# Block products of a gated network: sums of the seven products made by two wide additions, and one more pair of tiles in each network

## The chip, the cores and the metric

The kernel runs on one core of a Trainium2 chip. The metric is device time in microseconds (us) of one execution, the median of several runs. One further execution is recorded by the hardware profiler, and its trace is what the profile shows. Engines: PE (TensorE: matmuls; PEld is its weight load), DVE (VectorE), ACT (ScalarE), POOL (GpSimd) and SP (SyncE, which here issues DMAs).

## The reference, cut to what matters

Two residual layers on x of 512 tokens by 1024 channels. Each has a token mixer (first a state-space layer, then forgetting attention) and a gated network. The change lies in the two gated networks:

```python
def conv_ffn(h, w_up, conv_w, conv_b, w_down):
    up = h @ w_up
    a, b = jnp.split(up, 2, axis=-1)
    ...
    a_conv = conv_b
    for i in range(CONV_W):
        a_conv = a_conv + ap[:, i:i + S] * conv_w[i]
    return (jax.nn.silu(a_conv) * b) @ w_down
```

Here h is 512 by 1024 (normalised and modulated), w_up is 1024 by 5632, the convolution is causal with width 3 along the tokens, and w_down is 2816 by 1024.

## The kernel before, in words

Channels lie on the 128 partitions and tokens along the free dimension. All numbers are float32. To keep the precision, both operands of a matmul are split into a high part (rounded to the matmul's input format by a copy on ACT, line 301) and a low part (the difference, by a subtraction on DVE, line 302), and a product is three matmuls: high times high, high times low, low times high (lines 317 and 587).

The 2816 channels are 22 **pairs** of tiles: pair f is tile 2f (the half that is convolved) and tile 2f + 1 (the half that multiplies it). A pair is computed in one of two ways, chosen in `ffn` by the tuple `plain`, which lists the plain pairs.

- **Plain** (`product`, line 318): each tile is 8 blocks of 128 input channels, by three matmuls, of 512 tokens each: 24 matmuls of 512 columns, 48 a pair.
- **By block products** (`quarters`, lines 547 to 618): the pair's weights are seen as a 2 by 2 matrix of blocks, a11, a12 (the two halves of tile 2f's input channels) and a21, a22 (those of tile 2f + 1), and x as blocks b11, b12, b21, b22 (halves of the channels, by halves of the tokens, t1 and t2). Seven products of half the channels and half the tokens do in place of eight, after the method of Strassen and Winograd, with sums of weights s1 = a21 + a22, s2 = s1 - a11, s3 = a11 - a21, s4 = a12 - s2 and sums of x t1 = b12 - b11, t2 = b22 - t1, t3 = b22 - b12, t4 = t2 - b21. Each product is 12 matmuls of 256 columns. The four sums of weights are four DVE operations of 512 columns, and a11 with a12, s1 with s2, s4 with s3, and a22 are split into parts (three splits of 1024 columns and one of 512). The sums of x and their parts are made once in each network by `forms_x`, between the plain pairs at its start, ahead of the first pair by block products.

The results are: tile 2f is a11·b11 + a12·b21 for the first tokens and a11·b11 + s2·t2 + s1·t1 + s4·b22 for the second; tile 2f + 1 is a11·b11 + s2·t2 + s3·t3 - a22·t4 and a11·b11 + s2·t2 + s3·t3 + s1·t1. In PSUM, p1 gathers a11·b11, then s2·t2, then s3·t3, and p5 gathers s1·t1, then s4·b22. Since p1 and p5 go on gathering, what they hold in between is copied out by ACT (`copy`, line 594): after a11·b11, after s1·t1 and after s2·t2; p4 is copied as well. DVE then adds in four operations of 256 columns, each with one operand in PSUM (lines 607, 611, 616, 617, all recorded at line 555). `p1`, `p5`, `p2` and `p4` are in four PSUM tiles, of which the left half is used: two from `mm`, two from `aux` (four banks each). `oa` and `ob`, the sums in SBUF, share two buffers under the name nm_t.

`finish` is `gated`, lines 633 to 656: tile 2f is convolved (ACT at line 637, twice DVE at 639, ACT's Silu at 642), tile 2f + 1 multiplies it (DVE, 649), and the product is split into ghi and glo for w_down.

The pairs are in groups (`QGROUPS`, one tuple for each network). While the pairs of group q are computed, the products with w_down of group q - 1 are put between them (`down`, line 693): eight tiles of output a group, each with 3 matmuls of 512 columns for every pair in the group, spread evenly over the pairs of the next group. The first group has none between its pairs; those of the last group come at the end (line 696). Their results are added to the residual stream h by DVE (line 400).

The order on each engine in this part isn't written out by hand. Instructions carry the order of the program as priority, and a scheduler lays out each engine's queue ahead of time, by its own model of durations, letting a later instruction go ahead of one that isn't ready. On the chip each queue then runs in that order. `behind` (lines 182 to 187) adds waits for the order's sake: the parts of a pair's weights come after the copy of s2·t2 of the pair before (`self.copied`).

In network 1 DVE also makes 24 sums for the modulation of later layers (line 271), some after each product (`tick`). Weights come by DMA from SP's queue into three buffers named raw (in network 1 those of w_down into one named rawd).

Lines that the change and the prediction touch: 43 (`QGROUPS`), 301 and 302 (splits), 318 (plain products and w_down), 513 to 545 (`forms_x`), 547 to 618 (`quarters`), 633 to 656 (`gated`), 676 to 696 (the loop over pairs), 1797 and 1811 (the two networks, with `plain`).

Of the kernel before, what the change touches and what calls it, by code (L numbers as in the profile page):

```python
# [9 lines left out]
F32 = mybir.dt.float32  # L10
F32R = mybir.dt.float32r
I32 = mybir.dt.int32
AF = mybir.ActivationFunctionType
ALU = mybir.AluOpType
# [4 lines left out]
P = 128  # L19
D = 1024  # L20
KT = D // P
S = 512
# [17 lines left out]
WARM = 11  # L40

GROUPS = (11, 11)
QGROUPS = ((4, 4, 5, 4, 5), (6, 5, 6, 5))
TAIL = 6
FIRST = (("c", (KT,)), ("s5_prm", (3, G // 2)), ("s5_eye", (64,)), ("s5_causal", (L,)))
REST = (
# [27 lines left out]
def part_of(pool, shape, name, tag, bufs, aside=0):  # L74

    _, n, w = shape
    t = pool.tile([P, ROOM if bufs == WB else n * w + P], F32R, name=name, tag=tag, bufs=bufs)
    return t[:, aside:aside + n * w].rearrange("p (n w) -> p n w", w=w)


class Trunk:
# [465 lines left out]
    def quarters(self, pool, l, f, x, finish):  # L547

        nc = self.nc
        H, N = KT // 2, S // 2  # L550
        t1, t2 = HALVES
        a, b = (self.raw([P, KT, P], self.io["w_up"][l][2 * f + j]) for j in range(2))
        a11, a12, a21, a22 = a[:, :H], a[:, H:], b[:, :H], b[:, H:]
        c, d = (pool.tile([P, 2, H, P], F32, name="sums", bufs=2) for _ in range(2))
        sub = lambda o, u, v, op=ALU.subtract: nc.vector.tensor_tensor(o, u, v, op)  # L555
        w = {}
        copied = self.copied

        def parts(src, names, *where):
            hi, lo = (  # L560
                pool.tile([P, H * P + P], F32R, name=n, tag="e" + n)[:, ASIDE:ASIDE + H * P].rearrange("p (n w) -> p n w", w=P)
                if where else part_of(self.wpool, [P, len(names) * H, P], n, n, WB, ASIDE)
                for n in ("w_hi", "w_lo")
            )
            with self.behind(*copied):
                self.put_parts(hi, lo, src)
            for j, n in enumerate(names):
                w[n] = hi[:, j * H:(j + 1) * H], lo[:, j * H:(j + 1) * H]

        parts(a, ("a11", "a12"))  # L570
        sub(c[:, 0], a21, a22, ALU.add)
        sub(c[:, 1], c[:, 0], a11)
        parts(c.rearrange("p n k m -> p (n k) m"), ("s1", "s2"))
        sub(d[:, 1], a11, a21)
        sub(d[:, 0], a12, c[:, 1])
        parts(d.rearrange("p n k m -> p (n k) m"), ("s4", "s3"))
        parts(a22, ("a22",), pool)
        quarter = lambda k, t: tuple(v[:, k * H:(k + 1) * H, t] for v in x)
        xs = {"b11": quarter(0, t1), "b21": quarter(1, t1), "b22": quarter(1, t2)}
        for n, v in self.tx.items():  # L580
            xs[f"t{n}"] = v

        def times(o, wn, xn, first=True):
            (whi, wlo), (xhi, xlo) = w[wn], xs[xn]
            for k in range(H):
                for n, (wt, xt) in enumerate(((whi, xhi), (whi, xlo), (wlo, xhi))):
                    self.last_mm = nc.tensor.matmul(  # L587
                        o, wt[:, k], xt[:, k], start=(first and k == 0 and n == 0), stop=(k == H - 1 and n == 2),
                        skip_group_check=True,
                    )  # L590

        def copy(o, last=False):
            t = self.tmp.tile([P, N], F32, name="nm_h", bufs=4)
            a = nc.scalar.activation(t, o, AF.Copy)  # L594
            if last:
                self.copied = [a.ins]
            return t

        p1, p5 = (self.mm.tile([P, S], F32, name="mmp")[:, :N] for _ in range(2))
        p2, p4 = (self.aux.tile([P, S], F32, name="aux")[:, :N] for _ in range(2))  # L600
        oa, ob = (self.tmp.tile([P, S], F32, name="nm_t") for _ in range(2))
        times(p1, "a11", "b11")
        c1 = copy(p1)
        times(p5, "s1", "t1")
        c5 = copy(p5)
        times(p2, "a12", "b21")
        sub(oa[:, t1], p2, c1, ALU.add)
        times(p1, "s2", "t2", False)
        c2 = copy(p1, True)
        times(p5, "s4", "b22", False)  # L610
        sub(oa[:, t2], p5, c2, ALU.add)
        finish(2 * f, oa, slice(0, S))
        times(p4, "a22", "t4")
        c4 = copy(p4)
        times(p1, "s3", "t3", False)
        sub(ob[:, t2], p1, c5, ALU.add)
        sub(ob[:, t1], p1, c4)
        finish(2 * f + 1, ob, slice(0, S))

    def ffn(self, i, l, x, nxt, ticks=0, plain=None):  # L620

        nc, tc = self.nc, self.tc
        with tc.tile_pool(name=f"ffn{l}", bufs=1, reuse_waits="tile") as pool:
# [4 lines left out]
            cw, cb = conv[:, :3], conv[:, 3]  # L628
            groups = QGROUPS[l] if plain else GROUPS
            first = [sum(groups[:q]) for q in range(len(groups) + 1)]  # L630
# [86 lines left out]
class Ew:  # L717
# [29 lines left out]
    def sub(self, a, b, out=None):  # L747
        return self.tt(a, b, ALU.subtract, out)
# [1040 lines left out]
def build(tc, io, out, stop=None):  # L1789
    with ExitStack() as ctx:  # L1790
        k = Kernel(tc, io, ctx)
        x = k.s5(0, k.norm_mod(1))
        if stop == "s5":
            return k.dump(out)
        k.done()
        k.bg = [k.ada_units(units(*((2, t) for t in range(3))))]
        x = k.ffn(1, 0, x, k.norm_mod(2), ticks=1, plain=(0, 1, 2, 3, 6))
        k.done()
        k.bg = [
            k.ada_units(units((3, 1))[:7], rooms=("s3", "phi", "plo"), late=False),  # L1800
            k.ada_units(units((3, 1))[7:] + units((3, 0))[:6], rooms=(1, 2), late=False),
            k.ada_units(units((3, 0))[6:], rooms=("s3", "nf"), late=False),
        ]
        if stop == "ffn0":
            return k.dump(out)
        x = k.fox(2, x, k.norm_mod(3))
        k.done()
        k.mods.close()
        if stop == "fox":
            return k.dump(out)  # L1810
        k.ffn(3, 1, x, k.norm_out(out), plain=(0, 1, 2, 3))
        k.finish_norm()


# [81 lines left out]
```

## Time and profile before

| | |
|---|---|
| median of 3 runs | 1204.44 us (1204.01 to 1206.35) |
| profiled execution | 1204.63 us, of which its span, first to last instruction, 1202.8 us |
| granted PE clock, mean | 0.998 |
| pairs by block products | 17 in network 1 (plain: 0, 1, 2, 3, 6), 18 in network 2 (plain: 0 to 3) |
| network 1, about | 250 to 600 us of the span |
| network 2, about | 850 to 1200 us |

A row of a timeline gives start and duration in us, the engine, the line of the kernel, the operation, the tiles (output<-inputs) with their shapes, and a count; in brackets stands the idle time ahead of it with what ended it. Matmuls are pipelined and their ends are modelled, so PE's pace is read from starts. A row of a group ends with the busy time in us, the mean duration in ns, and the engine's idle time just ahead of these instructions with what ended most of it. A row of waits gives the total in us, the number of times and the longest.

### The profile page before, as it was taken

What the parts mean: (1) busy time and instruction counts of PE and PEld (TensorE: products, weight loads), DVE (VectorE), ACT (ScalarE), POOL (GpSimd) and SP (SyncE); (2) the same over time, 40 slices, a digit from 0 to 9 for tenths busy, and PEclk for the clock granted to TensorE, in tenths of its full rate; (3) what the DMA queues carried; (4) which work ended last, traced back from release to release, by engine and by line L of the source; (5) the groups of instructions that cost most, each with busy time, mean ns of one, the idle gap of its engine ahead of it and who ended that gap; (6) DMA issues with size and microseconds to landing.
All of it is one profiled execution on the core that took longest, in us unless ns stands there. A gap on an engine that the chain in (4) does not pass through costs nothing.

```text
span 1202.8 us, 20697 instructions
## 1 busy us (share of the span) xinstructions
PE 1179.2 (98%) x7947; PEld 1019.3 (85%) x7947; DVE 1010.3 (84%) x1843; ACT 615.7 (51%) x1179; POOL 124.5 (10%) x230
## 2 busy tenths in 40 slices
PE   9999999999999999999999999999999999999997
PEld 4576677898988899999899787878989999999987
DVE  8889887879899999998786678876899888888865
ACT  3565544436545544555452566664456555555543
POOL 3221011100000000000000344430000000000000
PEclk9999999999999999999999999999999999999999
DMA  9598677821465455433444444433123342323331
GB/s 370 190 348 282 197 247 253 280 71 53 142 191 162 143 169 181 142 112 88 140 169 167 150 149 150 142 113 102 59 70 97 123 125 86 110 88 110 112 100 71
DMA packets 71826, 182.00 MB, mean 151 GB/s; under 512 B 23103, under 2 KB 24479, under 8 KB 70703
## 3 DMA queue, kind: packets, MB, share of 16 engines
q1 hardware_dynamic: 58479, 136.63, 35.2%
q0 software_dynamic: 11920, 43.26, 10.6%
q8 instruction: 62, 1.02, 0.3%
q10 hardware_dynamic: 1328, 0.79, 0.2%
q14 instruction: 37, 0.30, 0.1%
HBM read 173.73 MB, written 6.92 MB: 150 GB/s over the span
## 4 chain that ended last, share of the span: by engine, by line
PE 60%; issue 19%; DVE 10%; DMA 7%; ACT 2%; POOL 1%; SPq 0%; DVEq 0%; POOLq 0%; ACTq 0%
PE mmp L318 25%; PE mmp L587 14%; PE aux L587 5%; PE mmp L1276 4%; DVE w_lo L302 3%; PE mmp L1616 2%; DMA raw<-in_ada_w 2%; PE aux L1034 1%; PE aux L1755 1%; DMA raw<-in_w_up 1%; PE mmp L227 1%; PE aux L1146 1%; PE aux L1775 1%; DMA ada_raw<-in_ada_t 1%; DMA rawd<-in_w_down 1%
## 5 line engine op out<-in xcount | busy, mean ns | idle before, releaser
L302 DVE TENSOR_TENSOR w_lo<-raw,w_hi 128x1024 fp32r<-128x1024 f32 (+4 forms) x173 | 186.1, 1080 | 26.5 <-ACT w_hi L301 26.1
L301 ACT ACTIVATE w_hi<-raw 128x1024 fp32r<-128x1024 f32 (+4 forms) x173 | 154.0, 899 | 86.7 <-PE mmp L318 35.4
L318 PE MATMUL mmp<-ghi,w_hi 128*128 128x512 f32 (+1 forms) x412 | 147.7, 359 | 0.7 <-DVE h L400 0.7
L318 PE MATMUL mmp<-ghi,w_lo 128*128 128x512 f32 (+1 forms) x412 | 147.3, 357 | 1.1 <-DVE w_lo L302 1.1
L318 PE MATMUL mmp<-glo,w_hi 128*128 128x512 f32 (+1 forms) x412 | 147.2, 357 | 0.0
L318 PE MATMUL mmp<-a_hi,w_hi 128*128 128x512 f32 (+1 forms) x320 | 116.5, 367 | 1.5 <-ACT a_hi L470 1.5
L587 PE MATMUL mmp<-w_hi 128*128 128x256 f32 x420 | 116.2, 277 | 0.8 <-ACT w_hi L301 0.4
L587 PE MATMUL mmp<-w_hi,w_lo 128*128 128x256 f32 x420 | 116.0, 277 | 0.0
L587 PE MATMUL mmp<-w_lo,w_hi 128*128 128x256 f32 x420 | 116.0, 276 | 0.0
L318 PE MATMUL mmp<-a_hi,w_lo 128*128 128x512 f32 (+1 forms) x320 | 114.3, 358 | 0.0
L318 PE MATMUL mmp<-a_lo,w_hi 128*128 128x512 f32 (+1 forms) x320 | 114.0, 357 | 0.0
L302 DVE TENSOR_TENSOR w_lo<-sums,w_hi 128x1024 fp32r<-128x1024 f32 x78 | 94.8, 1218 | 0.0
L301 ACT ACTIVATE w_hi<-sums 128x1024 fp32r<-128x1024 f32 x78 | 81.0, 1055 | 23.3 <-DVE sums L555 21.8
L594 ACT ACTIVATE nm_h<-mmp 128x256 f32<-128x256 f32 x105 | 39.6, 381 | 103.1 <-PE mmp L587 103.0
L318 PEld LDWEIGHTS mmp<-ghi,w_lo 128*128 128x128 f32 x412 | 77.4, 188 | 13.5 <-DVE w_lo L302 1.9
L318 PEld LDWEIGHTS mmp<-ghi,w_hi 128*128 128x128 f32 x412 | 77.3, 188 | 11.5 <-issue 0.9
L318 PEld LDWEIGHTS mmp<-glo,w_hi 128*128 128x128 f32 x412 | 77.4, 188 | 10.3
L587 PEld LDWEIGHTS mmp<-w_hi 128*128 128x128 f32 x420 | 78.8, 188 | 1.4 <-ACT w_hi L301 0.7
L587 PEld LDWEIGHTS mmp<-w_hi,w_lo 128*128 128x128 f32 x420 | 78.7, 188 | 0.4 <-DVE w_lo L302 0.2
L587 PE MATMUL mmp<-a_hi,w_hi 128*128 128x256 f32 x280 | 77.9, 278 | 1.1 <-ACT nm_h L594 0.9
L587 PEld LDWEIGHTS mmp<-w_lo,w_hi 128*128 128x128 f32 x420 | 78.8, 188 | 0.0
L587 PE MATMUL mmp<-a_hi,w_lo 128*128 128x256 f32 x280 | 77.7, 277 | 1.1 <-DVE w_lo L302 1.0
(339 smaller groups left out, 3128.3 us busy)
## 6 DMA issues: line engine op xcount, KB each, us to landing
raw<-in_w_up SPq DMA_DIRECT2D x88, 512.0 KB, 4.0
ada_raw<-in_ada_t POOLq DMA_DIRECT2D x40, 512.0 KB, 4.1
raw<-in_ada_w POOLq DMA_DIRECT2D x24, 512.0 KB, 6.3
nf<-nfd SPq DMA_DIRECT2D x8, 1152.0 KB, 7.0
raw<-in_ada_w SPq DMA_DIRECT2D x16, 512.0 KB, 9.8
raw<-in_fox_qk SPq DMA_DIRECT2D x16, 512.0 KB, 3.5
raw<-in_w_down SPq DMA_DIRECT2D x24, 320.0 KB, 3.0
rawd<-in_w_down SPq DMA_DIRECT2D x24, 256.0 KB, 3.4
```

The source lines that it names most:

```text
L227: self.last_mm = nc.tensor.matmul(ps[32 * qq:32 * qq + 32, :], self.sc32[:, k, :], w[:, q * S:(q + 1) * S], start=(step is steps[0]), stop ...
L301: self.rounded = nc.scalar.activation(hi, src, AF.Copy).ins
L302: return nc.vector.tensor_tensor(lo, src, hi.bitcast(F32), ALU.subtract)
L318: self.last_mm = self.nc.tensor.matmul(o if len(xt.shape) == 2 else by_place(o), wt, xt, start=(k == 0 and n == 0), stop=(k == nk - 1 and ...
L587: self.last_mm = nc.tensor.matmul(o, wt[:, k], xt[:, k], start=(first and k == 0 and n == 0), stop=(k == H - 1 and n == 2), skip_group_che ...
L594: a = nc.scalar.activation(t, o, AF.Copy)
L1034: nc.tensor.matmul(ps[:, :, cols], x[:, q, r].rearrange("p c j -> p (c j)"), both[:, :, planes, q, :], start=(r == 0), stop=(r == 1), skip ...
L1146: self.nc.tensor.matmul(yp[g2][:, k, 1:], w2[rows, k, r].rearrange("p c i -> p (c i)"), st[rows, r, k, :B - 1], start=False, stop=(r == 1) ...
L1276: one = lambda k: nc.tensor.matmul(ps, w[m][:, k, :], x[:, k], start=(k == 0), stop=(k == KT - 1))
L1616: self.last_mm = nc.tensor.matmul(ps[q, b][:, :n], xt[:, k, tb], wt, start=(k == 0 and i == 0), stop=(k == KT - 1 and i == 2),)
L1755: nc.tensor.transpose(pt[:, r - rs[0], k, :], s[:, r, k * P:(k + 1) * P], self.ident)
L1775: nc.tensor.matmul(pv[:, c * P:], self.v[:, hp, k, r].rearrange("p t d -> p (t d)"), pp[:, r, c + 3 * k:NB + 3 * k, :].rearrange("p b t -> ...
```

## The change

Three edits. In `quarters`, p2 and p5 become the two halves of one PSUM tile u, and p4 and p1 the two halves of one tile v; ACT copies straight into `oa` and `ob` (p4 with its sign turned), and two DVE operations of 512 columns make the sums in place, the second with p1 read twice by a broadcast. The four additions of 256 columns and the four small SBUF tiles of the copies go. In each network one pair more goes by block products: pair 6 in network 1, pair 3 in network 2. The groups of network 2 become 4, 6, 6, 6 pairs.

```diff
-QGROUPS = ((4, 4, 5, 4, 5), (6, 5, 6, 5))
+QGROUPS = ((4, 4, 5, 4, 5), (4, 6, 6, 6))
...
-        def copy(o, last=False):
-            t = self.tmp.tile([P, N], F32, name="nm_h", bufs=4)
-            a = nc.scalar.activation(t, o, AF.Copy)
-            if last:
-                self.copied = [a.ins]
-            return t
-
-        p1, p5 = (self.mm.tile([P, S], F32, name="mmp")[:, :N] for _ in range(2))
-        p2, p4 = (self.aux.tile([P, S], F32, name="aux")[:, :N] for _ in range(2))
+        def copy(t, o, scale=1.0):
+            return nc.scalar.activation(t, o, AF.Copy, scale=scale).ins
+
+        u, v = self.mm.tile([P, S], F32, name="mmp"), self.aux.tile([P, S], F32, name="aux")
+        p2, p5 = u[:, t1], u[:, t2]
+        p4, p1 = v[:, t1], v[:, t2]
         oa, ob = (self.tmp.tile([P, S], F32, name="nm_t") for _ in range(2))
         times(p1, "a11", "b11")
-        c1 = copy(p1)
+        copy(oa[:, t1], p1)
         times(p5, "s1", "t1")
-        c5 = copy(p5)
-        times(p2, "a12", "b21")
-        sub(oa[:, t1], p2, c1, ALU.add)
+        copy(ob[:, t2], p5)
+        times(p2, "a12", "b21", False)
         times(p1, "s2", "t2", False)
-        c2 = copy(p1, True)
+        self.copied = [copy(oa[:, t2], p1)]
         times(p5, "s4", "b22", False)
-        sub(oa[:, t2], p5, c2, ALU.add)
+        sub(oa, u, oa, ALU.add)
         finish(2 * f, oa, slice(0, S))
-        times(p4, "a22", "t4")
-        c4 = copy(p4)
+        times(p4, "a22", "t4", False)
+        copy(ob[:, t1], p4, -1.0)
         times(p1, "s3", "t3", False)
-        sub(ob[:, t2], p1, c5, ALU.add)
-        sub(ob[:, t1], p1, c4)
+        halves = lambda t: t.rearrange("p (n w) -> p n w", w=N)
+        sub(halves(ob), p1[:, None, :].to_broadcast([P, 2, N]), halves(ob), ALU.add)
         finish(2 * f + 1, ob, slice(0, S))
...
-        x = k.ffn(1, 0, x, k.norm_mod(2), ticks=1, plain=(0, 1, 2, 3, 6))
+        x = k.ffn(1, 0, x, k.norm_mod(2), ticks=1, plain=(0, 1, 2, 3))
...
-        k.ffn(3, 1, x, k.norm_out(out), plain=(0, 1, 2, 3))
+        k.ffn(3, 1, x, k.norm_out(out), plain=(0, 1, 2))
```

## The prediction

> **What bounds the kernel now.** The page comes first: its span, and the busy share of each engine.
>
> ```profile
> span 1202.8 us, 20697 instructions
> ...
> PE 1179.2 (98%) x7947; PEld 1019.3 (85%) x7947; DVE 1010.3 (84%) x1843; ACT 615.7 (51%) x1179; POOL 124.5 (10%) x230
> ```
>
> PE carries the span, with DVE close behind. The profiled execution took 1204.63 us, 1.8 us more than its span; the median of the runs shown is 1204.44 us, so a sum made against the one holds for the other. Next, PE's order of time where a plain tile ends and a block product begins (start, duration, engine, line, tiles, shapes).
>
> ```profile
> 297.16 0.39 PE L318 MATMUL mmp<-a_hi,w_lo 128*128 128x512 f32 x1
> ...
> 299.88 0.39 PE L318 MATMUL mmp<-a_hi,w_lo 128*128 128x512 f32 x1
> ...
> 301.37 0.28 PE L587 MATMUL mmp<-w_hi 128*128 128x256 f32 x1
> ...
> 302.73 0.28 PE L587 MATMUL aux<-a_hi,w_hi 128*128 128x256 f32 x1
> ```
>
> Durations overlap, so starts count. Twelve matmuls of 512 columns take 2.72 us, 0.2267 each; twelve of 256 columns 1.36 us, 0.1133 each. A plain pair has 48 of the first, 10.88 us; a pair by block products has 7 x 12 of the second, 9.52 us. **Each pair that changes over is worth 1.36 us of PE**, if PE has no wait. The windows by stage (length, busy time of PE, PEld, DVE, ACT, POOL with instructions, granted clock, DMA) tell where it hasn't.
>
> ```profile
> 320.00:340.00 20.00, 20.00 (x111) 17.32 (x110) 14.55 (x23) 7.20 (x11) 1.06 (x2) 1.00 0.66 217
> ...
> 400.00:420.00 20.00, 18.29 (x131) 16.69 (x129) 19.19 (x33) 11.64 (x20) 1.58 (x3) 1.00 0.38 123
> ...
> 880.00:900.00 20.00, 20.00 (x98) 16.69 (x97) 19.45 (x23) 9.95 (x14) 0.00 (x0) 1.00 0.25 71
> ```
>
> The first row is where network 1 now has its plain pair 6: DVE has 5.4 us to spare. In the second, DVE is 96% busy and PE loses 1.7 us. The last is the start of network 2: DVE is 97% busy, while plain pairs still keep PE full. PE is the bound, and DVE is as good as a second one in these places.
>
> **The change, part by part.** DVE's prices are read from starts in its order of time.
>
> ```profile
> 327.07 0.75 DVE L555 TENSOR_TENSOR nm_t<-mmp,nm_h 128x256 f32<-128x256 f32 x2
> 327.74 1.22 DVE L302 TENSOR_TENSOR w_lo<-raw,w_hi 128x1024 fp32r<-128x1024 f32 x1
> ...
> 334.28 1.29 DVE L555 TENSOR_TENSOR sums<-raw 128x512 f32<-128x512 f32 x2
> 335.48 0.69 DVE L555 TENSOR_TENSOR sums<-sums,raw 128x512 f32<-128x512 f32 x1
> ...
> 340.78 0.69 DVE L302 TENSOR_TENSOR w_lo<-rawd,w_hi 128x512 fp32r<-128x512 f32 x1 [2.74 <-ACT w_hi L301]
> ...
> 344.32 1.22 DVE L302 TENSOR_TENSOR w_lo<-sums,w_hi 128x1024 fp32r<-128x1024 f32 x1
> 345.46 0.68 DVE L649 TENSOR_TENSOR conv<-conv,mmp 128x512 f32<-128x512 f32 x1
> 346.06 1.22 DVE L302 TENSOR_TENSOR w_lo<-sums,w_hi 128x1024 fp32r<-128x1024 f32 x1
> ```
>
> *Two additions for four.* Now a pair has four additions of 256 columns, 0.34 us each from start to start (0.67 for the two); a 512-column operation with an operand in PSUM takes 0.60 (345.46 to 346.06). Two of those are 1.20 against 1.34: 0.14 us less DVE work in a pair, 5 us over the 35 pairs there are. PE waits for none of it directly, so I count it at nothing by itself. The broadcast operand of the second addition is in no row; between 0.60 and the 0.67 of two halves it doesn't matter. The copies on ACT stay four, of the same size.
>
> [...]
>
> *One more pair by block products in each network.* It takes two weight splits of 1024 away (2 x 1.14 us; 1.14 from 344.32 to 345.46) and brings three of 1024, one of 512 (0.60), four sums of 512 (0.60 each) and the two additions: 7.6 for 2.3, **5.3 us more DVE work** for 1.36 us less PE work.
>
> In network 1 it falls on pair 6. The 5.4 us of idle DVE take the work up, 2.74 us of it in the row at 340.78. But the stretch of the second window row comes right behind, where DVE is the bound, and DVE ends no earlier because PE arrives 1.36 us earlier. I count the gain there as given back, -1.36 + 1.36 = 0; bounds -1.4 (all taken up) and +2.6 (half of the 5.3 late).
>
> In network 2 the pair moved is number 3, the last plain one before block products begin.
>
> ```profile
> 890.33 1.22 DVE L302 TENSOR_TENSOR w_lo<-sums,w_hi 128x1024 fp32r<-128x1024 f32 x1
> 891.46 2.35 DVE L302 TENSOR_TENSOR w_lo<-raw,w_hi 128x1024 fp32r<-128x1024 f32 x2
> 893.73 0.74 DVE L639 SCALAR_TENSOR_TENSOR conv<-mmp,conv_wb,conv 128x511 f32<-128x511 f32 x1
> ...
> 897.46 1.23 DVE L302 TENSOR_TENSOR w_lo<-sums,w_hi 128x1024 fp32r<-128x1024 f32 x1
> ```
> ```profile
> 897.64 0.39 PE L318 MATMUL mmp<-a_hi,w_lo 128*128 128x512 f32 x1
> 897.87 0.28 PE L587 MATMUL mmp<-a_lo,w_hi 128*128 128x256 f32 x1
> ```
>
> The row at 890.33 splits the last of the four sums of x (forms_x); until then DVE is full. Plain pair 3 ends on PE at 897.87, so pair 2 ends 10.88 us before, at 887.0. There PE would now need pair 3's block weights, and nothing else is at hand: the first group has no products of w_down behind it. Without the two plain splits of 1.14 the forms are done near 890.3. From the end of the last plain split (891.46 + 2 x 1.14, less the block pair's first split: 892.6) to s1's low part at 898.7 lie 6.1 us, of which 1.3 are the two steps of another pair's convolution (the first is the row at 893.73): 4.8. So s1 is ready near 895.1, and from there six products (8.16 us) run to 903.2, where the plain pair ended at 897.87: **+5.3 us**. If DVE makes pair 3's weights ahead of the last two forms (4 x 1.14 us earlier) it is +0.8. The trace's order follows the program's, forms first; I take +4.
>
> *One bank for two products.* p2 and p5 now lie in one tile, p4 and p1 in another. Twice in a pair PE writes into a tile from which ACT is still copying the other half: p2 behind the copy of p5, s3·t3 behind the copy of p4. No row has this case. If order goes by columns it costs nothing. If it goes by tile, PE waits for the copy. One row of PE's waits has it held for a copy out of the tile that it writes, so I take the latter.
>
> ```profile
> PE mmp L587 <- ACT nm_h L594: 1.2, 2, 0.9
> ```
> ```profile
> 302.93 0.39 ACT L594 ACTIVATE nm_h<-mmp 128x256 f32<-128x256 f32 x1 [0.45 <-PE mmp L587]
> ```
>
> [...]
>
> This is the copy behind s1·t1, whose last matmul started at 302.62 (one before 302.73): it ends at 303.32, and the next product starts at 302.73 today. So p2 would start 0.6 us late, 37 x 0.6 = 22 us, unless PE has other work. It has: s2·t2 goes to the other tile, and its operands are split with s1. I take 0, and keep the 22 for the range. For s3·t3 the copy isn't punctual (all rows from ACT's groups, 292 to 1160 us):
>
> ```profile
> L301 ACT ACTIVATE w_hi<-sums 128x1024 fp32r<-128x1024 f32 x75 | 77.9, 1055 | 23.0 <-DVE sums L555 21.8 <-DVE sums L532 0.9
> ...
> L637 ACT ACTIVATE conv<-nm_t,conv_wb 128x512 f32<-128x512 f32 x35 | 28.4, 811 | 24.9 <-DVE nm_t L555 24.8
> ...
> L594 ACT ACTIVATE nm_h<-aux 128x256 f32<-128x256 f32 x35 | 12.8, 365 | 0.1
> ```
>
> The copy of p4 (last row) has 0.1 us of idle ACT before it in 35 cases: it always stands in ACT's queue behind something, namely the convolution's first step and the next pair's w_hi, and these wait 24.8 and 21.8 us for DVE. Today nobody waits for that copy but DVE. **Now PE would**: these 46.6 us become PE's, less what PE is given to do in between (products of w_down) and less what DVE gains while PE stands (a late pair makes the next one's weights early). Between 0 and 46.6 I take a tenth, 4.7: the order is laid out ahead and fills the waits that it foresees, and only lateness beyond that is left. About 1 us of the old wait in that row goes.
>
> *Groups of 4, 6, 6, 6.* The same 22 pairs, the same 32 tiles of w_down, the same matmuls. Six instead of five in the last group moves 8 x 3 matmuls of 0.2267, 5.4 us of PE, from among the pairs to the end, where nothing needs cover: DVE loses cover among the pairs. Counted within the terms above.
>
> **Sum**: network 1, 0; network 2's start, +4; waits for the bank, +4.7; old wait, -1. 1204.6 + 7.7 = **1212.3 us**.
>
> **The rivals.**
> - *All covered* (faster). The order puts pair 3's weights ahead and fills both waits: -2 x 1.36, and the 1.2 us of old waits: 1204.6 - 2.7 - 1.2 = 1200.7. For it: PE is held for ACT's copies only twice today, and each product of w_down (12 matmuls and more of 0.2267) is 2.7 us of filling. It decides if s1 of pair 3 is ready by 891 and ACT copies p4 ahead of the convolution. That the program doesn't wait by bank at all ends in the same place. Chance 0.30.
> - *Only network 2's start counts*, with DVE early enough: -1.36 + 0.8 to 2 and waits of 0 to 1: about 1204.6, no change. Chance 0.14.
> - *Nothing covered*: -2.7 + 5.3 + 22 + 46.6: 1276. Against it: matmuls of w_down stand behind most pairs. Chance 0.06.
> - The forecast, slower by 2.5 to 25 us: 0.50.
>
> **How the numbers follow.** About 0.2%, 2.4 us, is what a measurement can tell from no change. Faster 0.30, same 0.14, slower 0.56. The likeliest case's own range is 1207 to 1230; with the faster rival in, 1199 to 1230 leaves out the uncovered case and thin ends.
>
> **What would show it.** In the new trace: (1) a gap of PE of 2 to 8 us near 887, ended by w_lo or w_hi of pair 3; none means that the network 2 term is wrong. (2) PE L587 waiting for ACT's copies 10 or more times with over 3 us in all; none means that the bank term is wrong. (3) between p5 and p2, matmuls of s2·t2 or of w_down on PE; if PE idles there instead, the third rival holds. (4) in network 1, a PE as little busy as now in the 20 us of the second window row, or less; if it is full there, DVE's 5 us were worth more than nothing, and the forecast is too high.

## The result, and the profile after

| | before | after |
|---|---|---|
| median of 5 runs each | 1204.01 us (1202.4 to 1206.35) | 1232.42 us (1231.62 to 1233.36) |
| ratio, 95% interval | | 1.0236 (1.022 to 1.0252) |
| pairs by block products | 35 | 37 |
| granted PE clock, mean | 0.998 | 0.995 |

The changed kernel is slower by 28.4 us. The forecast was 1212.3 us with a range up to 1230: the direction is right, the size is not. In the page of the changed kernel the span and the busy shares are these.

```profile
span 1231.6 us, 20792 instructions
...
PE 1197.8 (97%) x8037; PEld 1026.1 (83%) x8037; DVE 1021.5 (83%) x1789; ACT 621.2 (50%) x1191; POOL 124.6 (10%) x230
```

PE seems as full as before (97% against 98%), and busy for 18.6 us longer, though two pairs fewer are plain, which should take 2.7 us off it. The lower clock (0.995 for 0.998) is worth at most some 3.7 us of that (0.003 x 1231.6). The ends of matmuls are modelled, so PE's records can hide waits. The weight loads show them: 26.8 us behind copies, 3.8 in PE's rows. First PE's own waits in the changed kernel (total in us, times, longest), then those of PEld, the weight load.

```profile
PE aux L587 <- ACT nm_t L593: 3.8, 8, 1.2
PE aux L587 <- DVE w_lo L302: 3.5, 1, 3.5
PE mmp L587 <- ACT w_hi L301: 3.2, 2, 2.3
```
```profile
PEld aux L587 <- ACT nm_t L593: 18.3, 39, 1.6
PEld mmp L587 <- ACT nm_t L593: 8.5, 33, 0.3
...
PEld aux L587 <- DVE w_lo L302: 3.7, 1, 3.7
PEld mmp L587 <- ACT w_hi L301: 3.7, 2, 2.5
```

L593 is the copy out of PSUM. By PE's view it holds PE 8 times for 3.8 us; by the weight loads 72 times (39 + 33, about two in each of the 37 pairs) for 26.8 us. The same view of the kernel before has one row for the copies:

```profile
PEld mmp L587 <- ACT nm_h L594: 1.6, 2, 1.1
```

One pair of network 2 shows what such a wait looks like. The changed kernel's order of time, PE, then PEld, then ACT (start, duration, engine, line, tiles):

```profile
970.51 0.28 PE L587 MATMUL mmp<-w_hi,w_lo 128*128 128x256 f32 x1
970.62 0.28 PE L587 MATMUL aux<-w_hi 128*128 128x256 f32 x1
...
970.96 0.28 PE L587 MATMUL aux<-w_hi 128*128 128x256 f32 x1
971.32 0.39 PE L587 MATMUL mmp<-a_hi,w_hi 128*128 128x256 f32 x1
971.54 0.28 PE L587 MATMUL mmp<-a_lo,w_hi 128*128 128x256 f32 x1
971.66 0.28 PE L587 MATMUL mmp<-a_hi,w_lo 128*128 128x256 f32 x1
```
```profile
970.85 0.19 PEld L587 LDWEIGHTS aux<-w_hi 128*128 128x128 f32 x1
971.32 0.19 PEld L587 LDWEIGHTS mmp<-a_hi,w_hi 128*128 128x128 f32 x1 [0.28 <-ACT nm_t L593]
```
```profile
970.88 0.38 ACT L593 ACTIVATE nm_t<-mmp 128x256 f32<-128x256 f32 x1 [0.51 <-PE mmp L587]
```

The last matmul of s1·t1 starts at 970.51. The scheduler did foresee the wait: it put four matmuls of s2·t2 (tile aux) between p5 and p2, as the prediction hoped. But these four and the one at 970.51 last 0.56 us together, and the copy of p5 ends at 970.88 + 0.38 = 971.26, 0.75 us after 970.51. So p2 starts at 971.32 instead of 971.07: 0.25 us. Its first matmul then takes 0.22 instead of 0.11 until the next one starts, and its weights weren't loaded ahead: elsewhere the load starts some 0.1 us before its matmul (970.85 for 970.96), here both start at 971.32. The pair has lost 0.35 us, and PE's row at 971.32 shows no idle time. All 33 waits of tile mmp are p2 behind the copy of p5, none over 0.3 us. Of the 39 of tile aux, which have the larger sum, most are s3·t3 behind the copy of p4.

The start of network 2, where pair 3 now goes by block products, in PE's order of time of the changed kernel:

```profile
893.85 0.28 PE L587 MATMUL aux<-a_lo,w_hi 128*128 128x256 f32 x1
897.66 0.38 PE L587 MATMUL aux<-a_hi,w_lo 128*128 128x256 f32 x1 [3.54 <-DVE w_lo L302]
...
899.02 0.41 PE L587 MATMUL aux<-a_hi,w_lo 128*128 128x256 f32 x1
901.69 0.58 PE L587 MATMUL mmp<-w_hi 128*128 128x256 f32 x1 [2.25 <-ACT w_hi L301]
```

PE stands for 3.54 and 2.25 us, first for the low part of a11 and a12, then for s1. And the windows behind the first wait (length, busy PE, PEld, DVE, ACT, POOL, then granted clock) show a cost that no term of the forecast held:

```profile
899.00:901.00 2.00, 0.44 (x3) 0.14 (x1) 1.97 (x4) 0.80 (x2) 0.00 (x0) 0.50 0.17 14
901.00:903.00 2.00, 1.27 (x5) 0.98 (x5) 1.60 (x3) 1.59 (x2) 0.00 (x0) 0.50 0.79 249
903.00:905.00 2.00, 2.00 (x9) 2.00 (x10) 2.00 (x3) 0.00 (x0) 0.00 (x0) 0.50 0.44 138
```

Behind the wait the granted clock is 0.50: the last 2 us hold 9 matmuls, where 18 would fit at 0.1133 each.

### The profile page after: what moved, and what is told of

It is laid out like the page before. It is cut to its first block, busy times and chain, and to the rows that moved or that the text cites. A ratio compares the mean times of both kernels' runs of the same rounds, so it can differ in the third digit from the quotient of the medians.

```text
span 1231.6 us, 20792 instructions
## 1 busy us (share of the span) xinstructions
PE 1197.8 (97%) x8037; PEld 1026.1 (83%) x8037; DVE 1021.5 (83%) x1789; ACT 621.2 (50%) x1191; POOL 124.6 (10%) x230
## 5 line engine op out<-in xcount | busy, mean ns | idle before, releaser
L318 PE MATMUL mmp<-ghi,w_hi 128*128 128x512 f32 (+1 forms) x418 | 148.8, 356 | 0.0
L318 PE MATMUL mmp<-glo,w_hi 128*128 128x512 f32 (+1 forms) x418 | 148.6, 355 | 0.0
L318 PE MATMUL mmp<-ghi,w_lo 128*128 128x512 f32 (+1 forms) x418 | 148.4, 355 | 0.0
L587 PE MATMUL aux<-w_hi 128*128 128x256 f32 x444 | 127.2, 287 | 4.6 <-ACT nm_t L593 3.8
L587 PE MATMUL aux<-w_hi,w_lo 128*128 128x256 f32 x444 | 123.4, 278 | 0.0
L587 PE MATMUL aux<-w_lo,w_hi 128*128 128x256 f32 x444 | 123.3, 278 | 0.0
L318 PE MATMUL mmp<-a_hi,w_hi 128*128 128x512 f32 (+1 forms) x288 | 104.1, 365 | 1.5 <-ACT a_hi L470 1.5
L593 ACT ACTIVATE nm_t<-aux 128x256 f32<-128x256 f32 x111 | 41.8, 377 | 122.3 <-PE aux L587 122.2
L318 PE MATMUL mmp<-a_hi,w_lo 128*128 128x512 f32 (+1 forms) x288 | 101.8, 354 | 0.0
L318 PE MATMUL mmp<-a_lo,w_hi 128*128 128x512 f32 (+1 forms) x288 | 101.7, 354 | 0.0
L587 PEld LDWEIGHTS aux<-w_hi 128*128 128x128 f32 x444 | 83.5, 188 | 18.5 <-ACT nm_t L593 18.3
L587 PE MATMUL mmp<-a_hi,w_hi 128*128 128x256 f32 x296 | 85.9, 290 | 2.0
L318 PEld LDWEIGHTS mmp<-ghi,w_lo 128*128 128x128 f32 x418 | 78.5, 188 | 10.5
L318 PEld LDWEIGHTS mmp<-ghi,w_hi 128*128 128x128 f32 x418 | 78.5, 188 | 9.8 <-ACT w_hi L301 0.4
L318 PEld LDWEIGHTS mmp<-glo,w_hi 128*128 128x128 f32 x418 | 78.5, 188 | 8.9
L587 PEld LDWEIGHTS aux<-w_lo,w_hi 128*128 128x128 f32 x444 | 83.6, 188 | 0.1
L587 PEld LDWEIGHTS aux<-w_hi,w_lo 128*128 128x128 f32 x444 | 83.5, 188 | 0.0
L587 PE MATMUL mmp<-a_hi,w_lo 128*128 128x256 f32 x296 | 82.2, 278 | 0.0
```

What stands on the lines that cost most here:

```text
L318: self.last_mm = self.nc.tensor.matmul(o if len(xt.shape) == 2 else by_place(o), wt, xt, start=(k == 0 and n == 0), stop=(k == nk - 1 and ...
L587: self.last_mm = nc.tensor.matmul(o, wt[:, k], xt[:, k], start=(first and k == 0 and n == 0), stop=(k == H - 1 and n == 2), skip_group_che ...
L593: return nc.scalar.activation(t, o, AF.Copy, scale=scale).ins
```

## The experiments

All stand beside runs of the kernel before. A cost in us is the ratio less 1, times 1204. "Old" and "new" name what the kernel before and the changed kernel have.

### Which edit costs the time

**e1**: the new `quarters`, with the old pairs and groups.

```diff
-        k.ffn(3, 1, x, k.norm_out(out), plain=(0, 1, 2))
+        k.ffn(3, 1, x, k.norm_out(out), plain=(0, 1, 2, 3))
...
-QGROUPS = ((4, 4, 5, 4, 5), (4, 6, 6, 6))
+QGROUPS = ((4, 4, 5, 4, 5), (6, 5, 6, 5))
```

(Against the changed kernel; network 1 has `plain=(0, 1, 2, 3, 6)` again.)

> The new block products (two PSUM tiles, two additions of 512 columns) with the old choice of pairs and groups. Theory A (PE waits by bank for ACT's copies, twice in a pair, and each wait costs about 0.65 us of weight load that cannot be pulled ahead): 35 pairs x 0.65 = 23 us more than before, 1222 to 1230 us, and PEld waits for nm_t of line 593 about 70 times. Theory B (the loss comes from the pairs and groups): within 3 us of before, 1201 to 1207.

Measured: 1230.35 us, ratio 1.0204 (1.0177 to 1.023), +24.6 us. **e2** is the rest: old `quarters`, new pairs and groups.

```diff
-        x = k.ffn(1, 0, x, k.norm_mod(2), ticks=1, plain=(0, 1, 2, 3, 6))
+        x = k.ffn(1, 0, x, k.norm_mod(2), ticks=1, plain=(0, 1, 2, 3))
...
-        k.ffn(3, 1, x, k.norm_out(out), plain=(0, 1, 2, 3))
+        k.ffn(3, 1, x, k.norm_out(out), plain=(0, 1, 2))
...
-QGROUPS = ((4, 4, 5, 4, 5), (6, 5, 6, 5))
+QGROUPS = ((4, 4, 5, 4, 5), (4, 6, 6, 6))
```

> The old block products with the new choice of pairs and groups. Theory A: the pair more in each network saves 2.7 us of PE, the start of network 2 loses 6 to 7 us of PE waiting for the first block pair's weights near 893: 1206 to 1211 us. Theory B: most of the 28 us, 1222 to 1232.

Measured: 1221.69 us, 1.0137 (1.0112 to 1.0163), +16.5 us. So the sums alone cost nearly all of it, and yet the pairs alone cost 16.5 more than nothing: 24.6 + 16.5 = 41.1 is well over the 28.4 of both together. The costs overlap. Waits of PEld in e2:

```profile
PEld mmp L587 <- DVE w_lo L302: 7.7, 16, 2.1
...
PEld mmp L587 <- ACT w_hi L301: 7.3, 9, 1.6
PEld mmp L318 <- DVE w_lo L302: 5.8, 7, 1.6
```

In e2 PE waits for weights that DVE and ACT make late. In the changed kernel PE stands for copies instead, and the first of these rows is down to

```profile
PEld mmp L587 <- DVE w_lo L302: 3.5, 5, 1.0
```

with one wait of 3.7 us more, at network 2's start, in the row of tile aux above. That DVE catches up while PE stands is a reading of these rows; no run shows it alone.

The three parts of e2 were then run one by one. **e5**: only pair 6 of network 1 by block products.

```diff
-        x = k.ffn(1, 0, x, k.norm_mod(2), ticks=1, plain=(0, 1, 2, 3, 6))
+        x = k.ffn(1, 0, x, k.norm_mod(2), ticks=1, plain=(0, 1, 2, 3))
```

> Kernel before with pair 6 of network 1 by block products, nothing else. Forecast of the prediction: no change (gain of 1.36 us given back), 1203 to 1206. Rival (DVE is the bound from 300 to 580 us, so its 5.3 us more come out at the end): 1208 to 1214.

**e6**: only pair 3 of network 2.

```diff
-        k.ffn(3, 1, x, k.norm_out(out), plain=(0, 1, 2, 3))
+        k.ffn(3, 1, x, k.norm_out(out), plain=(0, 1, 2))
```

> Kernel before with pair 3 of network 2 by block products, groups unchanged. The prediction: PE waits at the start of network 2 for s1, +4 us: 1207 to 1211. Rival (weights come early enough): 1203 to 1205.

**e7**: only the groups.

```diff
-QGROUPS = ((4, 4, 5, 4, 5), (6, 5, 6, 5))
+QGROUPS = ((4, 4, 5, 4, 5), (4, 6, 6, 6))
```

> Kernel before with groups of 4, 6, 6, 6 in network 2, nothing else. The prediction counts it at nothing: 1203 to 1206. Rival (fewer products of w_down between the pairs leave DVE without cover): over 1208.

| | median, us | ratio (95%) | cost, us |
|---|---|---|---|
| e5, pair 6 | 1210.99 | 1.0054 (1.0031 to 1.0078) | +6.5 |
| e6, pair 3 | 1209.99 | 1.0043 (1.0023 to 1.0064) | +5.2 |
| e7, groups | 1204.04 | 1.0009 (0.999 to 1.0027) | none |

Pair 6 costs more than its bound of 2.6; pair 3 costs what was forecast, 4 with an upper end of 5.3; the groups cost nothing. The three add up to 11.7, and e2's 16.5 is 4.8 more. Part of that is likely the clock. In e2's trace it is low in three stretches:

```profile
436.00:442.00 6.00, 5.19 (x22) 4.30 (x22) 4.64 (x7) 0.63 (x1) 0.00 (x0) 0.72 0.48 141
593.00:599.00 6.00, 5.41 (x33) 5.44 (x34) 3.99 (x9) 2.19 (x5) 0.00 (x0) 0.72 0.19 54
903.00:909.00 6.00, 5.47 (x31) 5.27 (x32) 4.78 (x6) 1.82 (x5) 0.00 (x0) 0.72 0.31 104
```

The last column but two is the clock. Against full clock each stretch lacks 0.28 x 6 = 1.7 us, nearly all with PE at work: an estimated 5 us of that execution. Its mean clock, 0.994 for the 0.998 of the kernel before, gives as much (0.004 x 1222.6 = 4.9 us). e5's mean is 0.998, that of the kernel before. e6's is 0.995, which gives some 3.6 us (0.003 x 1211.1); an estimated 1.7 of them are at the start of network 2 (its windows are shown further down). In e5 PE waits longer for w_lo in the plain products, those of w_down among them (row of PEld's waits):

```profile
PEld mmp L318 <- DVE w_lo L302: 6.7, 9, 1.7
```

and the same view of the kernel before:

```profile
PEld mmp L318 <- DVE w_lo L302: 3.0, 6, 1.3
```

DVE has 5.3 us more to do, in a network where the kernel before keeps it busy for 19.0 to 19.7 of every 20 us from 340 to 460, and part of it comes out in PE's waits for weights.

### Which piece of the new sums

**e8**: the kernel before with the shared tiles alone; old copies, four additions, old order.

```diff
-        p1, p5 = (self.mm.tile([P, S], F32, name="mmp")[:, :N] for _ in range(2))
-        p2, p4 = (self.aux.tile([P, S], F32, name="aux")[:, :N] for _ in range(2))
+        u, v = self.mm.tile([P, S], F32, name="mmp"), self.aux.tile([P, S], F32, name="aux")
+        p2, p5 = u[:, t1], u[:, t2]
+        p4, p1 = v[:, t1], v[:, t2]
```

(p2 and p4 also start with `False`, as in the change.)

> Kernel before with p2 and p5 in one PSUM tile and p4 and p1 in another, all else as before: four additions of 256 columns, copies into their own small tiles, old pairs and groups. Theory A (the shared tile makes PE wait for ACT's copies, and that alone is the loss of the new block products): within 4 us of the run with the new block products and the old pairs (1230): 1224 to 1234, PEld waiting for nm_h about 70 times. Rival (the early hold of nm_t and the later, wider additions cost): under 1212.

Measured: 1230.45 us, 1.0217 (1.0176 to 1.0258). The shared tiles alone are the whole loss of e1 (1.0204). The weight loads of e8 wait for the copies as in the changed kernel:

```profile
PEld aux L587 <- ACT nm_h L594: 20.0, 37, 1.5
PEld mmp L587 <- ACT nm_h L594: 9.8, 33, 2.5
```

**e9** is the other half: wide additions, with p2 and p5 in one tile (the first wide addition needs it), but p1 and p4 in tiles of their own, and two products laid between p5's copy and p2.

```diff
-        p4, p1 = v[:, t1], v[:, t2]
+        p4, p1 = self.aux.tile([P, S], F32, name="aux")[:, :N], v[:, :N]
...
         copy(ob[:, t2], p5)
-        times(p2, "a12", "b21", False)
+        times(p4, "a22", "t4")
+        copy(ob[:, t1], p4, -1.0)
         times(p1, "s2", "t2", False)
         self.copied = [copy(oa[:, t2], p1)]
+        times(p2, "a12", "b21", False)
         times(p5, "s4", "b22", False)
```

(Against the changed kernel; a22 is split ahead of s4 and s3, and pairs and groups are old.)

> The two wide additions with p2 and p5 in one PSUM tile, but p1 and p4 each in its own, old pairs and groups, products in the order a11 b11, s1 t1, a22 t4, s2 t2, a12 b21, s4 b22, s3 t3: between a copy and the next product into its tile lie two products (2.7 us). Theory A (waits by tile, with ACT's queue late by up to 3 us): nearly all of the loss goes, 1199 to 1206, and what is left below 1204 is DVE's gain of 5 us in network 1. Rival (the wide additions or the early hold of nm_t cost by themselves): over 1212.

Measured: 1204.52 us, 1.0008 (0.9987 to 1.0029). The loss is gone; the wide additions by themselves neither cost nor gain. To tell the two waits apart, **e12** keeps only that of p2: e9's three tiles, in the changed kernel's order.

```diff
         copy(ob[:, t2], p5)
-        times(p4, "a22", "t4")
-        copy(ob[:, t1], p4, -1.0)
+        times(p2, "a12", "b21", False)
         times(p1, "s2", "t2", False)
         self.copied = [copy(oa[:, t2], p1)]
-        times(p2, "a12", "b21", False)
         times(p5, "s4", "b22", False)
```

(Against e9; p4 comes behind s4·b22 again, a22 is split last.)

> The wide additions with the changed kernel's order of products, p4 in a tile of its own, old pairs: of the two waits in a pair only p2 behind the copy of p5 is left. If each wait costs its share, 1213 to 1220 (35 x 0.35 us); if the late copy of p4 is all that costs, within 3 us of before; if p2's wait is all, 1226 or more.

Measured: 1226.75 us, 1.0196 (1.0177 to 1.0215), +23.6 us: with p2's wait alone the kernel loses nearly as much as e1. (The wide additions are in e12 too; but e1 with them and e8 without them, in the same order, cost the same.) Divided by 35 pairs it is 0.67 us each, more than the 0.35 of the ordinary pair shown above, since some waits are long and the clock falls behind them. One of them, in e12's order of time on ACT and on PEld:

```profile
350.78 0.63 ACT L301 ACTIVATE w_hi<-rawd 128x512 fp32r<-128x512 f32 x1 [3.76 <-DMA rawd<-in_w_down]
351.32 0.37 ACT L593 ACTIVATE nm_t<-mmp 128x256 f32<-128x256 f32 x1
```
```profile
351.73 0.29 PEld L587 LDWEIGHTS mmp<-a_hi,w_hi 128*128 128x128 f32 x1 [3.52 <-ACT nm_t L593]
```

In ACT's order the copy of p5 stands behind the split of a tile of w_down whose DMA lands late (ACT idle 3.76 us), so p2 waits 3.52 us for a transfer with which it has nothing to do. In the windows of e12 the clock is low behind it (0.62), and again some 75 us later (0.66). The row of waits for p5's copy follows:

```profile
350.00:359.00 9.00, 7.26 (x38) 7.27 (x39) 4.17 (x8) 3.18 (x5) 0.53 (x1) 0.62 0.31 98
425.00:435.00 10.00, 8.52 (x36) 7.33 (x37) 7.84 (x10) 3.36 (x6) 0.53 (x1) 0.66 0.42 131
```
```profile
PEld mmp L587 <- ACT nm_t L593: 10.5, 29, 3.5
```

Against full clock the windows lack 0.38 x 9 + 0.34 x 10 = 6.8 us, of which an estimated 6, those with PE at work, are lost time. With the waits of 10.5 us and an estimated 0.1 us more at each of the 29 restarts (0.22 for 0.11 at 971.32 in the changed kernel) that is some 19 of the 23.6 us; the rest isn't accounted for. In e8, which has the same wait, the clock falls less: its mean is 0.997 to 0.998 in e8's four executions, 0.992 to 0.995 in e12's four.

**e14** keeps only the wait of s3·t3: the kernel before, with p4 and p1 in one tile.

```diff
-        p1, p5 = (self.mm.tile([P, S], F32, name="mmp")[:, :N] for _ in range(2))
-        p2, p4 = (self.aux.tile([P, S], F32, name="aux")[:, :N] for _ in range(2))
+        p2, p5 = (self.mm.tile([P, S], F32, name="mmp")[:, :N] for _ in range(2))
+        v = self.aux.tile([P, S], F32, name="aux")
+        p4, p1 = v[:, t1], v[:, t2]
```

(p4 also starts with `False`.)

> The kernel before with only p4 and p1 in one tile (p2 and p5 in tiles of their own), the old order, copies and additions: the wait of s3 t3 behind the copy of p4 alone. Theory C (the cost of a shared tile hangs on what lies behind the copy in the order laid out; here the scheduler has products of w_down for it, and e1 less e12 gives 3.6 us): 1205 to 1209; the forecast's term would make it 1208.7. Rival D (every product behind a copy out of its own tile costs the same 0.67 us a pair as p2 behind p5): 35 x 0.67, 1225 to 1230.

Measured: 1217.12 us, 1.0104 (1.0084 to 1.0124), +12.5 us, between the two theories: neither the 3.6 that e1 less e12 gives nor p2's price. The forecast's term for it was 4.7. Its mechanism is as the forecast had it; e14 on ACT, then on PE:

```profile
971.92 1.06 ACT L301 ACTIVATE w_hi<-sums 128x1024 fp32r<-128x1024 f32 x1 [1.38 <-DVE sums L555]
972.98 0.81 ACT L638 ACTIVATE conv<-nm_t,conv_wb 128x512 f32<-128x512 f32 x1
973.70 0.36 ACT L594 ACTIVATE nm_h<-aux 128x256 f32<-128x256 f32 x1
```
```profile
971.61 0.28 PE L587 MATMUL aux<-w_hi,w_lo 128*128 128x256 f32 x1
...
972.19 0.39 PE L318 MATMUL mmp<-ghi,w_lo 128*128 128x512 f32 x1
974.11 0.39 PE L587 MATMUL aux<-w_hi 128*128 128x256 f32 x1 [1.53 <-ACT nm_h L594]
```

p4 is done with the matmul at 971.61. Its copy starts at 973.70, behind the next pair's w_hi (which waited for DVE) and the convolution. Three matmuls of w_down, the last at 972.19, fill part of it, and PE stands for 1.53 us. The row of such waits in e14 is

```profile
PEld aux L587 <- ACT nm_h L594: 22.9, 34, 2.2
```

Both waits together (e8, +26.1) cost 10 us less than one by one (23.6 + 12.5). The waits themselves shrink little, from 22.9 to 20.0 us on tile aux and from 10.5 to 9.8 on tile mmp. By the estimate above, some 6 of the 10 us are the slow clock of e12 (mean 0.992 in its trace, 0.998 in e8's); the cause of the rest stays open. So each wait has two prices. p2's is 23.6 us alone and 13.6 on top of e14 (26.1 - 12.5); s3·t3's is 12.5 alone and 2.5 on top of e12 (26.1 - 23.6).

### Whether another order mends it

**e3** alternates the two tiles, so that a whole product (1.36 us) lies behind every copy: a11·b11, s1·t1, a22·t4, a12·b21, s2·t2, s4·b22, s3·t3. a22 is split ahead of s4 and s3. **e4** is the same with the old pairs and groups.

```diff
         copy(ob[:, t2], p5)
+        times(p4, "a22", "t4", False)
+        copy(ob[:, t1], p4, -1.0)
         times(p2, "a12", "b21", False)
         times(p1, "s2", "t2", False)
...
-        times(p4, "a22", "t4", False)
-        copy(ob[:, t1], p4, -1.0)
         times(p1, "s3", "t3", False)
```

> The changed kernel with the products in an order that alternates between the two PSUM tiles (a11 b11, s1 t1, a22 t4, a12 b21, s2 t2, s4 b22, s3 t3), a22 split earlier, so that each copy has a whole product of 1.36 us behind it before its tile is written again. Theory A: the bank waits go nearly all, about 24 us less than the changed kernel: 1206 to 1212 us. Rival (it is the later start of DVE's additions or the early hold of nm_t that costs): over 1220 us.

> The alternating order with the old choice of pairs and groups. Theory A: the 5 us less of DVE work are all that is left of the change: 1200 to 1205 us, the same as before or a little faster. Rival: over 1215 us.

Measured: e3 1229.01 us, 1.0197 (1.0172 to 1.0223); e4 1224.18 us, 1.0151 (1.0125 to 1.0176), +18.2. Both miss the theory that a product's distance is enough. In e4 the waits for copies are few, but long (PEld):

```profile
PEld aux L587 <- ACT nm_t L593: 11.9, 11, 3.4
```

The long ones are again copies behind a late tile of w_down in ACT's queue, as in e4's rows

```profile
488.36 0.74 ACT L301 ACTIVATE w_hi<-rawd 128x640 fp32r<-128x640 f32 x1 [5.77 <-DMA rawd<-in_w_down]
489.00 0.36 ACT L593 ACTIVATE nm_t<-aux 128x256 f32<-128x256 f32 x1
```

**e11** therefore puts the splits of w_down behind the pair's last copy, in e4's order.

```diff
-            with self.behind(*(late if m > ms[head] + 1 else ())):
+            with self.behind(*then, *(late if m > ms[head] + 1 else ())):
...
-                self.add_residual(i, q == last), after=after, ticks=0 if plain else ticks, **k
+                self.add_residual(i, q == last), after=after, ticks=0 if plain else ticks, then=self.copied, **k
```

> The alternating order (two tiles, old pairs), with the splits of w_down placed behind the pair's last copy on ACT, so that no copy stands behind a split that waits for its DMA. Theory A': what is left in the alternating order, 18 us, is ACT's copies held up in the queue by such splits; half or more goes: 1205 to 1215. Rival (the loss is in the waits themselves): 1220 to 1226, as without it.

Measured: 1239.89 us, 1.0303 (1.0285 to 1.0322), worse than all others, outside both expectations. PE now waits for high parts of weights, those of the block products (L587) above all, and those of w_down (L318):

```profile
PEld mmp L587 <- ACT w_hi L301: 7.7, 9, 1.2
...
PEld mmp L318 <- ACT w_hi L301: 4.3, 5, 1.2
```

The parts of the next pair's weights stand behind the same copy (`behind`), so both kinds of splits come to ACT at the same time; that this is why they are late is argued, not shown.

**e13** asks what the order itself costs: e4's order with four tiles, old copies and additions.

```diff
         parts(c.rearrange("p n k m -> p (n k) m"), ("s1", "s2"))
+        parts(a22, ("a22",), pool)
...
         parts(d.rearrange("p n k m -> p (n k) m"), ("s4", "s3"))
-        parts(a22, ("a22",), pool)
...
         c5 = copy(p5)
+        times(p4, "a22", "t4")
+        c4 = copy(p4)
         times(p2, "a12", "b21")
...
-        times(p4, "a22", "t4")
-        c4 = copy(p4)
         times(p1, "s3", "t3", False)
```

> The kernel before with the alternating order of the products (a11 b11, s1 t1, a22 t4, a12 b21, s2 t2, s4 b22, s3 t3; a22 split ahead of s4 and s3), but with four PSUM tiles of their own and the old copies and additions, so that no product waits for a copy of another. Theory C (in the alternating order too it is the shared tiles that cost, through copies that come late in ACT's queue): 1202 to 1209. Rival D (the order itself costs, a22 and p4 being early and s4 late): 1214 to 1226, near the 1224 of the alternating order with shared tiles.

Measured: 1212.09 us, 1.0058 (1.0043 to 1.0074), +7.0 us. It lies between the two expectations: of e4's 18.2, some 7 go with the order, and some 11 with the shared tiles, even at a product's distance. How the 11 divide between the copies behind late splits and other lateness isn't settled: e11 moved these splits and broke something else.

### The rest of the change, without the shared tiles

**e10** is e9 with pair 6 by block products; **e15** is e10 with pair 3 of network 2 and the new groups: the whole change, but for p4's own tile and the order of e9.

```diff
-        x = k.ffn(1, 0, x, k.norm_mod(2), ticks=1, plain=(0, 1, 2, 3, 6))
+        x = k.ffn(1, 0, x, k.norm_mod(2), ticks=1, plain=(0, 1, 2, 3))
```
```diff
-        k.ffn(3, 1, x, k.norm_out(out), plain=(0, 1, 2, 3))
+        k.ffn(3, 1, x, k.norm_out(out), plain=(0, 1, 2))
...
-QGROUPS = ((4, 4, 5, 4, 5), (6, 5, 6, 5))
+QGROUPS = ((4, 4, 5, 4, 5), (4, 6, 6, 6))
```

> The same with pair 6 of network 1 by block products as well. Theory A with DVE as the bound in network 1: DVE gets 5.3 us more than in the run before it and has got 2.5 less for its 17 pairs, so 3 us or less above that run: 1200 to 1209. Rival (pair 6 costs as much as in the kernel before): 6 us above that run.

> All of the change (one more pair in each network, groups 4, 6, 6, 6, wide additions), but with p4 and p1 in tiles of their own and two products between p5's copy and p2. Theory C (terms as measured alone add up once the shared tiles are gone: 1203.0 with pair 6, plus up to 5.2 for pair 3 of network 2, less what the wide additions give DVE there, plus 0 for the groups): 1203 to 1208. Rival D (a loss comes back with more pairs by block products): 1212 and more. Rival E (DVE's relief makes pair 3 a gain): 1199 to 1202, faster than both.

Measured: e10 1203.04 us, 0.9996 (0.9984 to 1.0008); e15 1209.84 us, 1.004 (1.0027 to 1.0054). With the new sums pair 6 costs nothing, where with the old ones it cost 6.5 us (e5). e10 differs from e5 by the wide additions and by the order, and which of the two gives DVE the room wasn't told apart. In costs, e15 (+4.8) is 5.3 us above e10 (-0.5), which is e6's price for pair 3; its median lies outside the expected 1203 to 1208. Between e15 and the changed kernel lie 23.6 us (28.4 - 4.8): that is what the tiles and the order of their products cost in the full change. No version was measurably faster than the kernel before.

## Why the prediction was wrong in size

The step that failed is the forecast's term for one bank with two products, 4.7 us, where the shared tiles alone cost 26.1 (e8). The larger miss is here: "So p2 would start 0.6 us late, 37 x 0.6 = 22 us, unless PE has other work. It has: s2·t2 goes to the other tile, and its operands are split with s1. I take 0, and keep the 22 for the range." The runs put 13.6 to 23.6 us in place of that 0 (e8 less e14, and e12). The fill was there, as sign (3) of the forecast asked, but the step priced it as if what the scheduler puts in covered what the chip then waits for. In the pair shown it laid out four matmuls (0.45 us) for a copy that ends 0.75 us after the product's last matmul starts, and from 970.96 to 971.32 PE started nothing. That the scheduler takes the copy for shorter than it is, is inferred from this order. At 70 of the 72 waits of the changed kernel PE also started again without a weight load ahead, which took an estimated 0.1 us more each. e12 comes near the forecast's 22 partly by luck: the ordinary wait is shorter, long ones behind late splits and the slow clock make up for it.

Point by point:

- **The bank.** That a half tile's copy holds the other half was right (e8: the tiles alone cost 1.0217). That the order laid out fills the wait was not: it holds for a part of each.
- **s3·t3 behind the copy of p4**: 4.7 was forecast, as a tenth of 46.6. It costs 12.5 alone (e14) and 2.5 on top of p2's wait, so the runs don't settle whether 4.7 was too low. The tenth had no row behind it. In the changed kernel the waits of tile aux, most of them of this kind, are 18.3 us against 8.5 for p2. The mechanism, the copy queued behind the convolution and w_hi, is in e14's rows.
- **Network 2's start**: +4, measured +5.2 (e6), in part by luck. s1's first matmul came at 894.77, where the forecast had 895.1. But PE did not stand until then, as the forecast had it ("nothing else is at hand"). It was given a22·t4, twelve matmuls from 887.31, and stood for 1.91 us, then for most of the 2 us from 895 (PE busy for 0.59). The slow clock behind the first gap (0.51 to 0.63), which the forecast hadn't, took an estimated 1.7 us (its windows are shown further down). PE's gap, expected near 887 by sign (1), is near 894 in the changed kernel, which is itself later by then, and is 3.54 + 2.25 us long.
- **Pair 6 of network 1**: 0 with bounds -1.4 and +2.6, measured +6.5 (3.7 to 9.4) with the old sums (e5), 0 in e10 against e9. The upper bound took half of DVE's 5.3 us as late; the loss is more than all of it.
- **Two additions for four**: 0.60 us each was right (the changed kernel: from 963.30 to 963.90 us, and with the broadcast from 967.02 to 967.62), and nothing by itself too. That they are off the path everywhere is not shown: e10 against e5 leaves room for more.
- **The groups**: 0, measured 0 (e7).
- **The signs**: (2) was written for PE's waits, "10 or more times with over 3 us": it shows 8 times and 3.8 us, as if the loss were small. The same waits are 72 times and 26.8 us in the weight loads. (4) asked whether the stretch from 400 to 420 would be fuller, and it is (PE busy for 19.74 us against 18.29), without the forecast being too high: busy time of PE includes hidden waits. It was no test.

Of the rivals, "nothing covered" (1276) put the two waits at their full 22 and 46.6. The first is near what p2's wait costs alone; the second isn't near.

## What to carry to other kernels

Before two accumulations share a PSUM tile, look for a copy out of one half that stands between writes to the other. In the changed kernel, with two such places in each of 37 pairs, the weight loads waited for ACT's copies 72 times and 26.8 us, though the columns are others. The waits were long where the copy stood behind other work in ACT's queue: 3.52 us in e12 behind a late split, 1.53 us in e14 behind w_hi and the convolution, against 0.28 us in the pair at 971.32. Price a wait that the scheduler is to fill by the real end of what is waited for, and not at nothing. To see short waits of a full PE, read the weight loads' waits, and compare sums of idle time there with those of the kernel before. Such a sum tells where to look, and is not the price: 22.9 us of waits cost 12.5 us in e14, and 10.5 us of them, with the slow clock behind, 23.6 us in e12.

## What the runs showed of the hardware

- The waits for copies cost more than their length. In the rows at 971.32 the load and its matmul start together and the next matmul comes 0.22 us later instead of 0.11: some 0.1 us beyond the lateness. Of the 72 such waits of the changed kernel, 70 end like this, with 0.22 or 0.23 us to the next start. In the other two the load came 0.06 us (at 348.01) and 0.11 us (at 372.35) ahead of its matmul, and the next start after 0.17 and 0.12.
- The granted clock fell to half behind some gaps of PE: to 0.50 in the changed kernel, with gaps of 3.54 and 2.25 us, and to 0.51 in e6. There PE stands for 1.91 us at the start of network 2:

```profile
890.75 0.39 PE L587 MATMUL mmp<-a_hi,w_lo 128*128 128x256 f32 x1 [1.91 <-DVE w_lo L302]
```

  The windows of e6 there are

```profile
889.00:891.00 2.00, 0.25 (x2) 0.26 (x3) 2.00 (x3) 1.04 (x1) 0.00 (x0) 1.00 0.00 0
891.00:893.00 2.00, 2.00 (x13) 2.00 (x13) 2.00 (x4) 0.34 (x1) 0.00 (x0) 0.63 0.00 0
893.00:895.00 2.00, 1.98 (x10) 1.69 (x9) 0.77 (x3) 1.10 (x2) 0.00 (x0) 0.51 0.44 94
895.00:897.00 2.00, 0.59 (x4) 0.39 (x4) 2.00 (x3) 1.06 (x1) 0.00 (x0) 1.00 0.55 184
```

  The clock is low for an estimated 3.5 us (2 at 0.51, and 0.37 / 0.5 of the 2 at 0.63), and while PE has work about half of that time is lost: matmuls of 256 columns start 0.21 us apart at 892 us, for 0.1133 where it is 1.00. In the changed kernel it is low for some 6.8 us, about twice as long, from 898.6 to 905.4. A gap of 1.91 us was enough in e6; in e14 the clock is 1.00 in both windows from 974 to 978, behind the gap of 1.53 us. A gap's length alone doesn't decide it: PE's waits in e8 have a longer one,

```profile
PE mmp L587 <- ACT nm_h L594: 2.6, 2, 2.4
```

  and the mean clock of that execution is 0.998, as in the kernel before, where e6's is 0.995.
- Costs don't add up: 24.6 and 16.5 us apart became 28.4 together, and 23.6 and 12.5 became 26.1. An experiment that does one part alone gives the price of that part alone, and its share in the whole comes from the run that leaves it out. The slow clock (mean 0.992 in e12's trace, 0.998 in e8's) is an estimated 6 of the 10 us that the second pair comes short.
